# Other start addresses for the split activations and weights of a two-block kernel on one core

## The chip, the cores and the metric

The kernel runs on one NeuronCore of one Trainium2 chip. The metric is the device time of one execution in microseconds (us). The kernel before has a median of 3423.22 us over three runs (3422.39 to 3428.16).

## The reference

Two network blocks are applied to a sequence of 1024 tokens of width 1024 (and 256 context tokens), in float32. The first has a mixer with two branches (a chunked spatial MLP and a gated linear attention over chunks of 64) and a SwiGLU layer; the second has a linear recurrence with a short convolution, a banded attention with 16 heads, and again a SwiGLU layer. Cut to what matters here, it is a series of large products of activations with weights:

```python
u_l, v_l, q_l, k_l, vv_l, r_l, af_l, ab_l, ga_l, gb_l = jnp.split(h_lat @ w_in, offs, axis=-1)
...
x = x + g1 * mix_l
x = x + g2 * _swiglu(_modulate(_rmsnorm(x, norm2_g[l]), sh2, sc2), w_ffn_in[l], w_ffn_out[l])
...
def _swiglu(h, w_ffn_in, w_ffn_out):
    a, g = jnp.split(h @ w_ffn_in, 2, axis=-1)
    return (jax.nn.silu(g) * a) @ w_ffn_out
```

## The kernel before

Each float32 operand of a large product is split into two float32r parts, `hi` (a rounded copy, by ScalarE) and `lo` (the rest, a subtraction on GpSimd or VectorE). A product is then three matmuls for each 128 rows of the inner dimension: hi by hi, the activations' lo by the weights' hi, hi by the weights' lo. `gemm` (L158 to L167) does this with a weight tile as the stationary operand, 128 columns wide, and an activation tile of 512 columns as the moving one; `gemm_tok` (L169 to L177) has the activations as the stationary operand and 256 weight columns as the moving one. `product` in the first half of the feed-forward layer (L1051 to L1053) and in the second (L1264 to L1266) issue the same three matmuls inline.

The parts live in two pools. `hp` has 32 buffers named `hl`, of 512 float32r values in each partition (2048 bytes), which `part` and `hnew` hand out for activations; some activation parts are taken from other pools (`half`, 2048 bytes, and `slot`, 4096 bytes). `wp` has 4 buffers for each of two names, `wh` and `wl`, of 1024 values (4096 bytes), for weights: `unit` (L139 to L152) loads a weight block into a `raw` tile, copies it to `wh` and subtracts into `wl`; `parts` in the feed-forward layer (L1033) and `room` (L1195) take such a pair and use its two halves for two blocks. A pool's buffers stand back to back in each partition.

`wh[:, k]` is the weight block of inner index k. With a block width of 128 it begins 512 bytes behind the one before. One user has another width: `low_rank` (L553 to L562) multiplies with the gate weights `waf`, a `unit` of width 96, whose blocks begin 384 bytes apart; its loop is that of `gemm` with 8 values of k for each half of the tokens.

The order of the instructions on each engine is that in which the program issues them; which buffer a tile gets follows the order of requests. `bacc.Bacc` (L1856) reserves a scratch area of 16384 bytes in each partition at address 0 for DMA descriptors; with it, SBUF is full to within a few hundred bytes.

Of the kernel before, what the change touches and what calls it, by code (L numbers as in the profile page):

```python
# [10 lines left out]
F32R = mybir.dt.float32r  # L11
# [5 lines left out]
P = 128  # L17
# [14 lines left out]
HQ = 512  # L32
# [17 lines left out]
def hs(q):  # L50

    return slice(q * HQ, q * HQ + HQ)


class Prog:
# [54 lines left out]
        return self.gp.tile([P, HQ], dt, name="half")  # L110

    def part(self, dt=F32R):
        return self.hp.tile([P, HQ], dt, name="hl")

    def hnew(self, n=8):

        hi, lo = [[None, None] for _ in range(n)], [[None, None] for _ in range(n)]
        for q in QS:
            for k in range(n):
                hi[k][q] = self.hp.tile([P, HQ], F32R, name="hl")  # L120
                lo[k][q] = self.hp.tile([P, HQ], F32R, name="hl")
        return hi, lo

    def gnew(self, n, dt):
# [14 lines left out]
    def unit(self, src, kt=8, width=P, eng=None, raw=None, into=None):  # L139

        nc = self.nc
        self.loads += 1
        self.flush(False)
        n = kt * width
        v = lambda t: t[:, :n].rearrange("p (k c) -> p k c", c=width)
        r = v(self.raw.tile([P, 1024], F32, name="raw") if raw is None else raw)
        if src is not None:
            nc.sync.dma_start(r, src.rearrange("p (k c) -> p k c", c=width))
        hi, lo = (v(t) for t in into or [self.wp.tile([P, 1024], F32R, name=nm) for nm in ("wh", "wl")])
        nc.scalar.copy(hi, r)  # L150
        self.last_split = (eng or nc.gpsimd).tensor_tensor(lo, r, hi.bitcast(F32), op=ALU.subtract).ins  # L151
        return hi, lo  # L152
# [862 lines left out]
    def ffn_in(self, wi, hid):  # L1015


        nc = self.nc
        V = nc.vector
        add, sub = ALU.add, ALU.subtract  # L1020
        nf = FT

        def load(f, i, j):
            r = self.half()
            nc.sync.dma_start(r, wi[2 * f + i][:, hs(j)])
            return r

        def total(a, b, op):
            s = self.half()
            V.tensor_tensor(s, a, b, op=op)  # L1030
            return s

        def parts(*srcs):  # L1033
            hi, lo = (self.wp.tile([P, 1024], F32R, name=nm) for nm in ("wh", "wl"))
            out = []
            for i, s in enumerate(srcs):
                h, l = hi[:, hs(i)], lo[:, hs(i)]
                self.split(h, l, s, eng=nc.gpsimd)
                out.append([t.rearrange("p (k c) -> p k c", c=P) for t in (h, l)])
            return out  # L1040

        banks = [0]

        def product(w, n):
            mm = nc.tensor.matmul
            self.tick()
            banks[0] += 1
            o = self.mm_bank() if banks[0] % 2 else self.ax_bank()
            wh, wl = w
            for k, (h, l) in enumerate(self.X[n]):  # L1050
                mm(o, wh[:, k], h, start=k == 0, stop=False)  # L1051
                mm(o, wh[:, k], l, start=False, stop=False)  # L1052
                mm(o, wl[:, k], h, start=False, stop=k == 3)  # L1053
            return o

        def copied(a):
            t = self.half()
            nc.scalar.copy(t, a)
            return t

        def gate(a):
            s = self.t512()
            nc.scalar.activation(s, a, AF.Silu)
            return s

        def hidden(f, q, s, c):
            V.tensor_tensor(s, s, c, op=ALU.mult)
            self.store(hid[f][:, hs(q)], s)

        raws, todo, ready = {}, [], deque()  # L1070
        seen = [0]

        def ahead(f):

            self.loads += 1
            self.flush(False)
            for g in (f, f + 1):
                if g < nf and g not in raws and (g == f or f >= LEAD - 1):
                    raws[g] = [load(g, i, j) for i in QS for j in QS]
            a11, a12, a21, a22 = raws.pop(f)  # L1080
            s1 = total(a21, a22, add)
            s2 = total(s1, a11, sub)
            s3 = total(a11, a21, sub)
            s4 = total(a12, s2, sub)
            todo.extend([s2, s1, s3, a22, s4] if f < LEAD else [a11, s2, s1, s3, a22, a12, s4])

        def fill():
            while len(ready) < 7 and (todo or seen[0] < nf):
                while len(todo) < 2 and seen[0] < nf:
                    ahead(seen[0])  # L1090
                    seen[0] += 1
                ready.extend(parts(*todo[:2]))
                del todo[:2]

        def weights():
            fill()
            return ready.popleft()

        first = []
        for f, (w1, w2) in enumerate([parts(load(f, 0, 0), load(f, 0, 1)) for f in range(LEAD)]):  # L1100
            t = copied(product(w1, "B11"))
            s = total(t, product(w2, "B21"), add)
            nc.scalar.activation(s, s, AF.Silu)
            first.append((t, s))
            if not f:
                ahead(0)
                seen[0] = 1
        for f in range(nf):
            if f < LEAD:
                t, s0 = first[f]  # L1110
            else:
                t = copied(product(weights(), "B11"))
            u2 = total(t, product(weights(), "T2"), add)
            p5 = product(weights(), "T1")
            u3 = total(u2, product(weights(), "T3"), add)
            c22 = total(u3, p5, add)
            V.tensor_tensor(u2, u2, p5, op=add)
            V.tensor_tensor(u3, u3, product(weights(), "T4"), op=sub)
            if f >= LEAD:
                V.tensor_tensor(t, t, product(weights(), "B21"), op=add)  # L1120
                s0 = gate(t)
            hidden(f, 0, s0, u3)
            V.tensor_tensor(u2, u2, product(weights(), "B22"), op=add)
            hidden(f, 1, gate(u2), c22)

    def ffn_out(self, wo, hid, xs, scale, pieces, squares, norm, extra=lambda: iter(())):
# [3 lines left out]
        nc = self.nc  # L1130
# [64 lines left out]
        def room(w):  # L1195

            if not space:
                hi, lo = (self.wp.tile([P, 1024], F32R, name=nm) for nm in ("wh", "wl"))
                space.extend((hi[:, hs(i)][:, :w], lo[:, hs(i)][:, :w]) for i in QS)
            return space.pop(0)  # L1200

        def supply():

            for bi, ((kind, n), f0) in enumerate(zip(FF_BLOCKS, starts)):
# [17 lines left out]
                for p in range(4):  # L1222
                    self.loads += 1
                    self.flush(False)
                    raw = [self.raw.tile([P, 1024], F32, name="raw") for _ in QS]
                    for i in QS:
                        nc.sync.dma_start(raw[i][:, :n * P], wo[2 * p + i][:, cols])
                    (a11, a12), (a21, a22) = ((r[:, :w], r[:, w:2 * w]) for r in raw)

                    def done(src):  # L1230
                        hi, lo = room(w)
                        self.split(hi, lo, src, eng=nc.gpsimd)
                        return [t.rearrange("p (k c) -> p k c", c=P) for t in (hi, lo)], 1
                    yield done(a11)
                    yield done(a12)
                    s1 = self.t512()[:, :w]
                    V.tensor_tensor(s1, a21, a22, op=add)
                    V.tensor_tensor(a21, a11, a21, op=sub)
                    V.tensor_tensor(a11, s1, a11, op=sub)
                    V.tensor_tensor(a12, a12, a11, op=sub)  # L1240
                    for src in (s1, a11, a21, a22, a12):
                        yield done(src)
# [48 lines left out]
        for bi, (kind, nb) in enumerate(FF_BLOCKS[:-1]):  # L1291
# [19 lines left out]
            else:  # L1311
                for m in range(0, 8, 2):
                    t = self.t512()
# [553 lines left out]
```

## Time and profile before

| | |
|---|---|
| median of three runs | 3423.22 us |
| profiled execution, its own time | 3423.95 us |
| its span, first to last instruction | 3422.2 us |
| mean granted TensorE clock | 0.981 |
| TensorE matmul busy | 3260.1 us (95%), 15,868 |
| VectorE / ScalarE / GpSimd busy | 2126.6 / 1363.1 / 1539.2 us |
| DMA | 335.11 MB, mean 98 GB/s |

A matmul's length in the trace (0.39 us for 512 columns) is that of a pipelined instruction and overlaps the next one; the rate is read from the interval between starts. The rows PEld are TensorE's weight loads. A granted clock of 1.00 is 2.4 GHz, one of 0.50 is 1.2 GHz.

### The profile page before, as it was taken

The numbers are of one execution on the slowest core, as the hardware profiler recorded it, in microseconds if no ns is written. First come the engines' busy times: TensorE is split into PE (matmuls) and PEld (weight loads), VectorE is DVE, ScalarE is ACT, GpSimd is POOL, SyncE is SP. The second block draws the span as 40 slices with busy tenths as digits, with TensorE's granted clock in tenths as the row PEclk, the third lists the DMA queues.
The fourth block names the chain that finished last, engine by engine and source line by source line (L and its number), as shares of the span: only waits on it lengthen the run. The fifth ranks groups of instructions, "written<-read, shape, count | busy, mean of one in ns | idle before, by whom it ended". The sixth has DMA issues, their size and how long they took to land. (4 is left out here: it accounts for less than half of the span.)

```text
span 3422.2 us, 43238 instructions
## 1 busy us (share of the span) xinstructions
PE 3260.1 (95%) x15868; PEld 2695.3 (79%) x15868; DVE 2126.6 (62%) x3438; ACT 1363.1 (40%) x2396; POOL 1539.2 (45%) x991
## 2 busy tenths in 40 slices
PE   7999999999999999999989989999999999999998
PEld 4778888888888878888767867777777778888767
DVE  7554234333667386565798487777776585554786
ACT  4552122211122442222434486666665333233433
POOL 3222233221312775454655433444444775554764
PEclk9999999999999999999999999999999999999999
DMA  6121121244236522221342411111114422222342
GB/s 257 62 105 59 50 68 65 75 157 133 77 119 218 171 89 84 74 96 60 122 164 84 131 33 55 45 54 45 55 48 139 161 99 98 81 81 94 98 132 79
DMA packets 153012, 335.11 MB, mean 98 GB/s; under 512 B 20864, under 2 KB 29184, under 8 KB 152800
## 3 DMA queue, kind: packets, MB, share of 16 engines
q1 hardware_dynamic: 140640, 311.36, 27.5%
q10 hardware_dynamic: 12160, 20.98, 1.7%
q8 instruction: 126, 2.06, 0.3%
q14 instruction: 86, 0.70, 0.1%
HBM read 263.07 MB, written 69.21 MB: 97 GB/s over the span
## 5 line engine op out<-in xcount | busy, mean ns | idle before, releaser
L151 POOL TENSOR_TENSOR wl<-raw,wh 128x1024 fp32r<-128x1024 f32 (+1 forms) x188 | 426.1, 2271 | 742.7 <-ACT wh L150 666.1
L163 PE MATMUL mm<-hl,wh 128*128 128x512 f32 (+1 forms) x1584 | 636.8, 402 | 1.6 <-ACT t L1547 1.4
L165 PE MATMUL mm<-hl,wl 128*128 128x512 f32 (+1 forms) x1584 | 625.4, 395 | 2.8 <-POOL wl L151 2.8
L164 PE MATMUL mm<-hl,wh 128*128 128x512 f32 (+1 forms) x1584 | 624.2, 394 | 0.0
L193 POOL TENSOR_TENSOR wl<-half,wh 128x512 fp32r<-128x512 f32 x308 | 432.1, 1426 | 345.6 <-ACT wh L192 340.3
L150 ACT CAST wh<-raw 128x1024 fp32r<-128x1024 f32 (+3 forms) x189 | 177.3, 940 | 491.6 <-PE mm L164 215.7
L165 PEld LDWEIGHTS mm<-hl,wl 128*128 128x128 f32 (+1 forms) x1584 | 300.9, 190 | 68.0 <-POOL wl L151 3.6
L163 PEld LDWEIGHTS mm<-hl,wh 128*128 128x128 f32 (+1 forms) x1584 | 301.6, 190 | 59.5 <-ACT t L1547 1.8
L164 PEld LDWEIGHTS mm<-hl,wh 128*128 128x128 f32 (+1 forms) x1584 | 301.3, 190 | 58.1 <-issue 0.5
L192 ACT CAST wh<-half 128x512 fp32r<-128x512 f32 x308 | 178.5, 619 | 390.4 <-PE ax L1052 197.2
L1030 DVE TENSOR_TENSOR half<-half 128x512 f32<-128x512 f32 x176 | 204.4, 1200 | 3.0
L1606 POOL TENSOR_SCALAR p<-p,ast 128x384 f32<-128x384 f32 (+1 forms) x64 | 84.1, 1314 | 263.5 <-DVE ast L1604 172.5
L175 PE MATMUL mm<-wh,hl 128*128 128x256 f32 x576 | 166.1, 289 | 3.4 <-ACT wh L150 3.4
L177 PE MATMUL mm<-wl,hl 128*128 128x256 f32 x576 | 164.5, 286 | 1.9 <-POOL wl L151 1.9
L176 PE MATMUL mm<-wh,hl 128*128 128x256 f32 x576 | 164.5, 286 | 0.8 <-DVE hl L193 0.6
L1052 PE MATMUL mm<-hl,wh 128*128 128x512 f32 x360 | 140.6, 391 | 3.3 <-POOL hl L193 3.3
L1051 PE MATMUL mm<-hl,wh 128*128 128x512 f32 x360 | 140.3, 390 | 0.7 <-ACT hl L192 0.7
L1053 PE MATMUL mm<-hl,wl 128*128 128x512 f32 x360 | 140.3, 390 | 0.0
L1051 PE MATMUL ax<-hl,wh 128*128 128x512 f32 x344 | 134.2, 390 | 2.0 <-ACT hl L192 1.3
L1053 PE MATMUL ax<-hl,wl 128*128 128x512 f32 x344 | 134.1, 390 | 0.1
L1052 PE MATMUL ax<-hl,wh 128*128 128x512 f32 x344 | 133.9, 389 | 0.0
L193 POOL TENSOR_TENSOR wl<-raw,wh 128x384 fp32r<-128x384 f32 x96 | 113.1, 1198 | 39.4 <-ACT wh L192 38.8
(419 smaller groups left out, 7996.7 us busy)
## 6 DMA issues: line engine op xcount, KB each, us to landing
half<-in_w_fi SPq DMA_DIRECT2D x196, 256.0 KB, 4.8
hid<-t SPq DMA_DIRECT2D x78, 256.0 KB, 2.0
half<-hid SPq DMA_DIRECT2D x72, 256.0 KB, 4.5
raw<-in_w_ada SPq DMA_DIRECT2D x32, 512.0 KB, 3.8
raw<-in_w_o SPq DMA_DIRECT2D x32, 512.0 KB, 3.9
raw<-in_w_fo SPq DMA_DIRECT2D x32, 384.0 KB, 3.3
slot<-in_w_ada SPq DMA_DIRECT2D x16, 512.0 KB, 10.2
raw<-in_w_u SPq DMA_DIRECT2D x16, 512.0 KB, 3.7
```

Source lines behind the costliest of these rows:

```text
L150: nc.scalar.copy(hi, r)
L151: self.last_split = (eng or nc.gpsimd).tensor_tensor(lo, r, hi.bitcast(F32), op=ALU.subtract).ins
L163: mm(o, wh[:, k], h[k][q][:, s], start=k == 0, stop=False)
L164: mm(o, wh[:, k], l[k][q][:, s], start=False, stop=False)
L165: mm(o, wl[:, k], h[k][q][:, s], start=False, stop=k == kt - 1)
L175: mm(o, h[k][q][:, s], wh[:, k % 4], start=k == 0, stop=False)
L192: self.nc.scalar.copy(hi, x)
L193: (eng or self.nc.vector).tensor_tensor(lo, x, hi.bitcast(F32), op=ALU.subtract)
L1030: V.tensor_tensor(s, a, b, op=op)
L1051: mm(o, wh[:, k], h, start=k == 0, stop=False)
L1052: mm(o, wh[:, k], l, start=False, stop=False)
L1053: mm(o, wl[:, k], h, start=False, stop=k == 3)
```

## The change

Each buffer of `hp` becomes 12 values longer and each buffer of `wp` 16 values longer, and the tiles use only the first 512 or 1024 of them. So the buffers are spaced by 2096 and 4160 bytes, where they were spaced by 2048 and 4096. The descriptor scratch is halved to 8192 bytes, which gives the room for the padding. No instruction is added, removed or moved. Where a tile of either pool is asked for, the request goes through `part` or the new `wpart`.

```diff
     def part(self, dt=F32R):
-        return self.hp.tile([P, HQ], dt, name="hl")
+        return self.hp.tile([P, HQ + 12], dt, name="hl")[:, :HQ]
+
+    def wpart(self, name):
+        return self.wp.tile([P, 1024 + 16], F32R, name=name)[:, :1024]
...
-                hi[k][q] = self.hp.tile([P, HQ], F32R, name="hl")
-                lo[k][q] = self.hp.tile([P, HQ], F32R, name="hl")
+                hi[k][q], lo[k][q] = self.part(), self.part()
...
-        hi, lo = (v(t) for t in into or [self.wp.tile([P, 1024], F32R, name=nm) for nm in ("wh", "wl")])
+        hi, lo = (v(t) for t in into or [self.wpart(nm) for nm in ("wh", "wl")])
...
-            hi, lo = (self.wp.tile([P, 1024], F32R, name=nm) for nm in ("wh", "wl"))
+            hi, lo = (self.wpart(nm) for nm in ("wh", "wl"))
...
-    nc = bacc.Bacc("TRN2", target_bir_lowering=False, num_devices=1)
+    nc = bacc.Bacc("TRN2", target_bir_lowering=False, num_devices=1, dynamic_dma_scratch_size=8192)
```

The same replacement stands in `room`.

## Rows read from the trace of the kernel before

**Rows 1.** The page's first part: busy us (share of the span) and instructions by engine.

```profile
PE 3260.1 (95%) x15868; PEld 2695.3 (79%) x15868; DVE 2126.6 (62%) x3438; ACT 1363.1 (40%) x2396; POOL 1539.2 (45%) x991
```

**Rows 2.** Stretches: us, busy PE, PEld, DVE, ACT, POOL, granted clock, DMA share, GB/s.

```profile
1280.00:1600.00 320.00, 320.00 (x1413) 265.08 (x1412) 189.59 (x223) 94.14 (x167) 163.56 (x120) 1.00 0.24 81
1960.00:2600.00 640.00, 593.60 (x2844) 484.72 (x2843) 483.91 (x982) 438.16 (x827) 266.60 (x149) 0.97 0.16 50
...
2051.20:2053.80 2.60, 2.60 (x8) 2.00 (x7) 2.56 (x4) 1.41 (x2) 1.44 (x1) 0.50 0.00 0
1450.20:1455.90 5.70, 5.70 (x27) 4.69 (x25) 2.45 (x4) 1.68 (x3) 2.91 (x2) 1.00 0.04 14
```

**Rows 3.** Instructions in order of time (start us, length us), a steady stretch.

```profile
1450.23 0.39 PE L1051 MATMUL ax<-hl,wh 128*128 128x512 f32 x1
1450.23 0.19 PEld L1052 LDWEIGHTS ax<-hl,wh 128*128 128x128 f32 x1
...
1455.90 0.39 PE L1052 MATMUL ax<-hl,wh 128*128 128x512 f32 x1
```

**Rows 4.** In order of time, a stretch at the half clock.

```profile
2051.21 0.63 PE L163 MATMUL mm<-hl,wh 128*128 128x512 f32 x1
...
2053.77 0.63 PE L163 MATMUL mm<-hl,wh 128*128 128x512 f32 x1
```

**Rows 5.** TensorE's groups by line and shape: count, busy us, mean ns, idle before.

```profile
L163 PE MATMUL mm<-hl,wh 128*128 128x512 f32 x1568 | 630.5, 402 | 1.6 <-ACT t L1547 1.4 <-ACT wh L150 0.2
...
L1051 PE MATMUL ax<-hl,wh 128*128 128x512 f32 x344 | 134.2, 390 | 2.0 <-ACT hl L192 1.3 <-DVE half L1030 0.7
...
L1051 PE MATMUL ax<-half,wh 128*128 128x512 f32 x272 | 106.4, 391 | 0.0
```

**Rows 6.** In order of time, `low_rank` with 96 weight columns.

```profile
103.14 0.40 PE L163 MATMUL mm<-hl,wh 128*96 128x512 f32 x1
103.38 0.40 PE L164 MATMUL mm<-hl,wh 128*96 128x512 f32 x1
...
105.92 0.40 PE L163 MATMUL mm<-hl,wh 128*96 128x512 f32 x1
106.16 0.40 PE L164 MATMUL mm<-hl,wh 128*96 128x512 f32 x1
```

**Rows 7.** In order of time, 512-column products behind a run of other matmuls.

```profile
252.00 0.40 PE L163 MATMUL mm<-hl,wh 128*128 128x512 f32 x1
252.24 0.39 PE L164 MATMUL mm<-hl,wh 128*128 128x512 f32 x1
252.46 0.39 PE L165 MATMUL mm<-hl,wl 128*128 128x512 f32 x1
...
254.07 0.39 PE L163 MATMUL mm<-hl,wh 128*128 128x512 f32 x1
...
255.43 0.39 PE L163 MATMUL mm<-hl,wh 128*128 128x512 f32 x1
```

**Rows 8.** In order of time, products between the attention's small matmuls.

```profile
2097.41 0.40 PE L163 MATMUL ax<-slot,wh 128*128 128x512 f32 x1
...
2098.56 0.40 PE L165 MATMUL ax<-slot,wl 128*128 128x512 f32 x1
```

**Rows 9.** In order of time, products with 256 moving columns.

```profile
245.77 0.28 PE L175 MATMUL mm<-wh,hl 128*128 128x256 f32 x1
...
246.95 0.28 PE L176 MATMUL mm<-wh,hl 128*128 128x256 f32 x1
...
249.95 0.28 PE L177 MATMUL mm<-wl,hl 128*128 128x256 f32 x1
```

**Rows 10.** ScalarE's copies into the two pools, by line and shape.

```profile
L192 ACT CAST wh<-half 128x512 fp32r<-128x512 f32 x308 | 178.5, 619 | 390.4 <-PE ax L1052 197.2 <-issue 148.4 <-DVE half L1030 23.0
...
L192 ACT CAST hl<-half 128x512 fp32r<-128x512 f32 x76 | 45.9, 617 | 50.7 <-DVE half L1176 23.3 <-DVE half L338 11.4 <-DVE half L1181 7.0
```

**Rows 11.** The page's DMA queues: kind, packets, MB, share of 16 engines.

```profile
q1 hardware_dynamic: 140640, 311.36, 27.5%
q10 hardware_dynamic: 12160, 20.98, 1.7%
```

More of the change, by code (lines that the diff above doesn't have):

```diff
@@ L1197, in room @@
             if not space:
-                hi, lo = (self.wp.tile([P, 1024], F32R, name=nm) for nm in ("wh", "wl"))
+                hi, lo = (self.wpart(nm) for nm in ("wh", "wl"))
                 space.extend((hi[:, hs(i)][:, :w], lo[:, hs(i)][:, :w]) for i in QS)
```

## The prediction

> **What bounds the kernel now.** I read the busy times first, then a table of stretches, then single matmuls in order of time in the stretches where nothing is waited for. TensorE is busy for 3260.1 of 3422.2 us; VectorE has 62%, GpSimd 45%, ScalarE 40% [rows 1]. In the stretch 1280 to 1600 us TensorE has all 320.00 us while the next busiest engine has 189.59; in 1960 to 2600 it has 593.60 of 640 and VectorE 483.91, so some waiting is mixed in there [rows 2]. In steps of 40 us, 35 of 86 stretches are like the first. The chain of waits adds nothing: its last links are a short tail. So the time is mostly the number of matmuls times the interval from one matmul's start to the next, and a change of addresses alone, with the same instructions in the same order, can reach the time only through that interval, or through longer instructions on the engines that feed it.
>
> The interval in the steady stretch: from 1450.23 to 1455.90 us there are 25 intervals, (1455.90 - 1450.23) / 25 = 226.8 ns; each weight load starts together with the matmul before the one that needs it (both at 1450.23) and takes 0.19 us, so it is read from SBUF while that matmul streams its moving operand [rows 3]. The granted clock is 1.00 there, 2.4 GHz [rows 2], and 512 columns at 2.4 GHz are 213.3 ns, so some 13.4 ns of each interval are something else. Where the granted clock is 0.50, 1.2 GHz [rows 2], this is gone: six intervals from 2051.21 to 2053.77 are 426.7 ns each, exactly 512 / 1.2 [rows 4]. So the excess is not a fixed charge for each instruction in ns. It fits two reads that get into each other's way only when the engine streams at full speed, which is the case in which addresses could matter.
>
> **What the change touches.** The big kinds of matmul with a moving operand of 512 columns are L163 to L165 (1568 each with moving `hl`) and L1051 to L1053 (344 each with `hl` into `ax`, 272 with `half`, and as many again into `mm`) [rows 5]; with the smaller kinds of that shape in the same view they come to about 11,000 of the 15,868 matmuls. Nearly all have `wh` or `wl` as weights, and most have `hl` as the moving operand. Before, every buffer of the two pools begins at the same remainder modulo 512 bytes (spacings 2048 and 4096, slices by k 512 bytes apart). After, the remainder steps by 48 bytes from one `hl` buffer to the next, and by 64 bytes between weight buffers. Within one product the weights keep their remainder over k, `wh` and `wl` differ, and the moving one alternates between the two parts and moves on with k.
>
> **Where the trace shows other remainders.** One place: `low_rank` takes its weights 96 columns wide, so `wh[:, k]` steps by 384 bytes, and modulo 512 it runs through four remainders and repeats after 4 k, which is 12 matmuls. There the intervals do not settle. The twelve from 103.14 to 105.92 us take 2.78 us, 231.7 ns each, for narrower weights; and the lengths repeat with just that period: a pair with 0.40 us stands at 103.14 and 103.38, and the next such pair in the same place of the loop at 105.92 and 106.16, 2.78 us later, while matmuls in between show 0.39 [rows 6]. What has the period of 4 k in that loop is the weights' remainder alone. The second witness is a restart. After a run of other matmuls, with every remainder equal, the intervals are uneven for about nine matmuls, (254.07 - 252.00) / 9 = 230.0 ns, and then lock: (255.43 - 254.07) / 6 = 226.7 ns [rows 7]. Where the attention's small matmuls lie between, they never lock: (2098.56 - 2097.41) / 5 = 230.0 ns [rows 8]. So 226.7 is a settled state that is lost when the relation between the two reads is disturbed, and the unsettled state costs 3.3 to 5.0 ns more. After the change that relation is another one at nearly each step. For a moving operand of 256 columns the sign is the other way: unsettled (246.95 - 245.77) / 10 = 118 ns, settled (249.95 - 246.95) / 25 = 120 ns [rows 9]. It concerns some 1,900 matmuls (L175 to L177 and their like).
>
> **Sum.** Of the 11,000 about one in five is already unsettled (an estimate: the attention's 640 us hold 2844 of 15,868 matmuls, 18% [rows 1, 2], and restarts add a little). That leaves 8,800. At 230.0 they cost 8,800 x 3.3 = 29 us, at 231.7 they cost 8,800 x 5.0 = 44 us. I take 3.7 ns, nearer to the restart, since that has weights of the same 128 columns: 33 us. The 256-column ones give back 1,900 x 2 = 4 us. In the stretches where TensorE waits, part of a longer interval only shortens the wait; of the 29 us left I take off a tenth: 26. Bounds for a single interval are the uneven ones themselves: about 0.22 us (252.24 to 252.46) and 0.24 (252.00 to 252.24) [rows 7]. If all 11,000 went to 0.22 us the kernel would gain 11,000 x 6.7 = 74 us, if all went to 0.24 it would lose 11,000 x 13.3 = 146; no run of matmuls here stays at either, so these are outer bounds and not ends of the range.
>
> **What costs nothing.** ScalarE's copy into `wh` (128x512) takes 619 ns and the one into `hl` 617 [rows 10], the same for tiles of two pools; they lie under TensorE's work, as ScalarE is busy for 94.14 and GpSimd for 163.56 of the 320 us from 1280 [rows 2]. If each were 5% longer, that cover would still hold; where TensorE waits for a split (1960 to 2600) it would not, which at 5% of ScalarE's 438.16 us there is 22 us at the very most, and I see no reason for it. Pools, buffer counts, order of allocation and waits stay as they are, so no transfer starts at another point. The halved descriptor scratch makes room for the padding (32 x 48 + 8 x 64 = 2048 bytes); 140,640 of the 153,012 packets are on one hardware queue (q1, named hardware_dynamic), 12,160 on another like it [rows 11], and I cost it at nothing, with nothing gained either.
>
> **The skill against this.** The row shows that intervals depend on the weights' remainder. The Trainium skill says otherwise: "TensorE: Matmul & The Clock Gate", step-by-step of part 2, has two independent SBUF read ports for TensorE, so that loading the next weights takes no bandwidth from the running matmul, and "SBUF — State Buffer", section "Who interferes with whom", has TensorE never waiting on another engine. By that rule addresses would not matter and the time would stay at 3423; that is the first rival. The restart speaks for it, being uneven with equal remainders; the 12-matmul period speaks against it.
>
> **Rivals.**
> 1. Nothing changes (the padding doesn't do what it is for): the period of twelve is a property of 96-column weights, and the lock doesn't depend on addresses. For it: products with `hl` and with `half`, tiles in quite different places, have the same length in the mean, 390 and 391 ns [rows 5]. Against it: narrower weights alone give no reason for a period of 4 k. 3420 to 3428 us. Chance 0.22.
> 2. Faster: with unequal remainders the two reads meet less often, and the interval for 512 columns falls below 226.7, as the unsettled 256-column one falls below 120. Place: all products with `wh` and `wl`. Price: 2 ns as there, times 11,000 = 22 us, 3402. It decides from the point where the mean interval in the 1280 to 1600 stretch is under 226 ns. If the excess of 13.4 ns went altogether, as at the half clock, it would be 147 us (3277), and half of that if all stood at 0.22 us; no run at full clock comes near. Chance 0.20, 0.04 of it for these larger forms.
> 3. The lock survives within each product, because the weights keep their remainder there and the pairs of remainders repeat in order, and is only lost for a third of the matmuls: 29 / 3 = 10 us, 3434. Chance 0.16.
>
> **How the numbers follow.** Forecast: the lock is lost. The profiled execution took 3423.95 us around its span of 3422.2, 0.7 over the median of 3423.22; 3423.95 + 26 = 3450. Chance 0.42, own range 3440 to 3485, its upper end being 226.7 to 233 ns for all that is now locked (8,800 x 6.3 = 55 us) and a few us more. The range for all cases, 3402 to 3480, takes in no change and the small gain and leaves out the large gain and the worst loss, under 2 in 10. Under 0.2%, about 7 us, a measurement of this kernel can't be told from no change. Faster 0.20, same 0.22, slower 0.58.
>
> **What would show it.** Right: from 1280 to 1600 us (now 320.00 us of TensorE, all settled) the same 1413 matmuls take some 325 us, with intervals spread between 0.22 and 0.24 us and no lock; copies and splits keep their mean lengths; the clock stays 1.00 there. Rival 1: 226.7 ns as now. Rival 2: a mean under 226. Rival 3: uneven intervals only for a few matmuls at the head of each product. Wrong altogether if instructions of VectorE, ScalarE or GpSimd have other lengths, or waits on the feeding engines grow.

## The result, and the profile after

| | before | after |
|---|---|---|
| median of three runs, us | 3423.22 | 3444.12 (3442.51 to 3445.69) |
| profiled execution, its own time, us | 3423.95 | 3442.51 |
| its span, us | 3422.2 | 3440.7 |
| mean granted clock | 0.981 | 0.985 |

The ratio is 1.0057, with a 95% interval of 1.0034 to 1.008: slower by 21 us at the median and by 18.5 us in the span. The forecast was 3450, its own range 3440 to 3485. All 15,868 TensorE instructions run in the same order as before. Line numbers are two higher after: L165 to L167 are the old L163 to L165, L177 to L179 the old L175 to L177, and L1053 to L1055 the old L1051 to L1053.

First the page's busy line of the kernel after (busy us, share, instructions), beside [rows 1]:

```profile
PE 3283.1 (95%) x15868; PEld 2683.0 (78%) x15868; DVE 2126.6 (62%) x3438; ACT 1363.3 (40%) x2396; POOL 1543.2 (45%) x991
```

TensorE has grown by 23.0 us and GpSimd by 4.0; VectorE is the same to the tenth. The stretches of [rows 2], after:

```profile
1280.00:1600.00 320.00, 320.00 (x1385) 260.08 (x1384) 189.37 (x222) 91.66 (x162) 160.84 (x116) 1.00 0.24 82
...
1960.00:2600.00 640.00, 595.54 (x2844) 482.40 (x2844) 487.17 (x967) 437.11 (x817) 268.88 (x148) 0.98 0.15 49
```

In the first, which has no waits and a full clock, 1385 matmuls fit where 1413 did: each takes longer. In the second, with its waits, as many fit as before, 2844. There the granted clock was also a little higher, 0.98 against 0.97, so that line alone doesn't say whether the waits or the clock made up for the longer intervals; the table at the end of this section parts the two. Single matmuls in order of time (start us, length us), beside [rows 3]:

```profile
1453.01 0.39 PE L1054 MATMUL mm<-half,wh 128*128 128x512 f32 x1
...
1457.09 0.39 PE L1054 MATMUL ax<-half,wh 128*128 128x512 f32 x1
...
1457.55 0.40 PE L1053 MATMUL mm<-half,wh 128*128 128x512 f32 x1
...
1459.88 0.39 PE L1054 MATMUL mm<-half,wh 128*128 128x512 f32 x1
```

The interval is no longer one number. From 1453.01 it is (1457.09 - 1453.01) / 18 = 226.7 ns, as before; with the next weight buffer, from 1457.55, it is (1459.88 - 1457.55) / 10 = 233 ns. Over the matmuls that ran from 1280 to 1600 us before, the mean is 231.2 where it was 226.67. The groups of [rows 5] (mean ns of one), a 256-column stretch beside [rows 9], and ScalarE's copy into `wh` beside [rows 10]:

```profile
L165 PE MATMUL mm<-hl,wh 128*128 128x512 f32 x1568 | 633.2, 404 | 1.4 <-ACT t L1549 1.4
...
L1053 PE MATMUL ax<-half,wh 128*128 128x512 f32 x272 | 107.0, 393 | 0.0
```

```profile
249.10 0.28 PE L178 MATMUL mm<-wh,hl 128*128 128x256 f32 x1
...
251.93 0.28 PE L178 MATMUL mm<-wh,hl 128*128 128x256 f32 x1
```

```profile
L194 ACT CAST wh<-half 128x512 fp32r<-128x512 f32 x308 | 178.4, 618 | 403.9 <-PE ax L1054 209.6 <-issue 150.5 <-PE mm L166 19.7
```

Matmuls fed from `hl` and from `half` have both grown by some 2 ns in the length shown, though `half` was not moved: their weights were. With 256 columns the interval is (251.93 - 249.10) / 24 = 117.9 ns, where it was 120. The copy takes 618 ns where it took 619. At the half clock nothing has changed (beside [rows 4]): six intervals of (2063.65 - 2061.09) / 6 = 426.7 ns, exactly as before.

```profile
2061.09 0.63 PE L167 MATMUL mm<-hl,wl 128*128 128x512 f32 x1
...
2063.65 0.63 PE L167 MATMUL mm<-hl,wl 128*128 128x512 f32 x1
```

Where the time went, by stretches of the time before, matmul by matmul. "512 columns" and "256 columns" are the growth of all such intervals at full clock (215 to 245 ns, or 106 to 130 ns, in both traces), with the number of the first kind ahead of it. "Half clock" is the growth of all other intervals that a half-clock stretch touches in either trace, and "rest" that of what is left, nearly all of it intervals with a wait. "Shift" is by how much later the same matmuls run at the end of the stretch than at its start; it is the sum of the four, to rounding. All columns but the second are in us.

| stretch, us | intervals | 512 columns | 256 columns | half clock | rest | shift |
|---|---|---|---|---|---|---|
| 0 to 680 | 1378 | +4.3 | -1.9 | +1.6 | -0.4 | +3.5 |
| 680 to 960 | 705 | +2.5 | -1.7 | -1.1 | -0.3 | -0.5 |
| 960 to 1600 | 2661 | +11.3 | 0.0 | 0.0 | -0.4 | +10.8 |
| 1600 to 2800 | 3657 | +11.6 | -0.2 | -6.4 | -6.8 | -1.8 |
| 2800 to 3120 | 1412 | +6.3 | 0.0 | 0.0 | 0.0 | +6.3 |
| 3120 to the end | 913 | +3.5 | -0.3 | -2.5 | -0.5 | +0.3 |
| all | 10,726 | +39.4 | -4.1 | -8.4 | -8.4 | +18.6 |

The stretches in which TensorE hardly waits (960 to 1600 and 2800 to 3120 us, most of the two feed-forward layers) pass the growth on. The attention and what lies around it, 1600 to 2800 us, pass on none of it, for two reasons of like size: shorter waits, and less time at the half clock.

### The profile page after: what moved, and what is told of

It reads as the page before. It is cut to its first block, busy times and chain, and to the rows that moved or that the text cites. A ratio compares the mean times of both kernels' runs of the same rounds, so it can differ in the third digit from the quotient of the medians.

```text
span 3440.7 us, 43238 instructions
## 1 busy us (share of the span) xinstructions
PE 3283.1 (95%) x15868; PEld 2683.0 (78%) x15868; DVE 2126.6 (62%) x3438; ACT 1363.3 (40%) x2396; POOL 1543.2 (45%) x991
## 5 line engine op out<-in xcount | busy, mean ns | idle before, releaser
L165 PE MATMUL mm<-hl,wh 128*128 128x512 f32 (+1 forms) x1584 | 639.5, 404 | 1.4 <-ACT t L1549 1.4
L167 PE MATMUL mm<-hl,wl 128*128 128x512 f32 (+1 forms) x1584 | 627.7, 396 | 2.5 <-POOL wl L153 2.5
L167 PEld LDWEIGHTS mm<-hl,wl 128*128 128x128 f32 (+1 forms) x1584 | 299.8, 189 | 71.6 <-POOL wl L153 3.3
L165 PEld LDWEIGHTS mm<-hl,wh 128*128 128x128 f32 (+1 forms) x1584 | 300.2, 190 | 63.1 <-ACT t L1549 1.8
L177 PE MATMUL mm<-wh,hl 128*128 128x256 f32 x576 | 165.0, 287 | 3.3 <-ACT wh L152 3.3
L179 PE MATMUL mm<-wl,hl 128*128 128x256 f32 x576 | 163.4, 284 | 1.6 <-POOL wl L153 1.6
L1053 PE MATMUL mm<-hl,wh 128*128 128x512 f32 x360 | 141.8, 394 | 0.6 <-ACT hl L194 0.6
L1055 PE MATMUL mm<-hl,wl 128*128 128x512 f32 x360 | 141.6, 393 | 0.0
L1053 PE MATMUL ax<-hl,wh 128*128 128x512 f32 x344 | 135.8, 395 | 1.4 <-ACT hl L194 1.0
L1055 PE MATMUL ax<-hl,wl 128*128 128x512 f32 x344 | 135.4, 394 | 0.0
```

Of the source, the lines that this page charges most:

```text
L165: mm(o, wh[:, k], h[k][q][:, s], start=k == 0, stop=False)
L167: mm(o, wl[:, k], h[k][q][:, s], start=False, stop=k == kt - 1)
L177: mm(o, h[k][q][:, s], wh[:, k % 4], start=k == 0, stop=False)
```

## The experiments

In all kernels but the two small ones the computation is the whole one. A weight buffer's start minus a moving buffer's start, modulo 256 bytes, is called the difference below; before, it is 0 for all products in question. The `hl` buffers of the changed kernel lie 2112 bytes apart, not the 2096 that were asked for; the intervals of the kernel with only the activations spaced show it, below. So all differences in the changed kernel are multiples of 64: 0, 64, 128 or 192.

### One difference at a time

Small kernel: it leaves the computation out and only issues groups of 48 matmuls on three tiles, groups following without a break, at a granted clock of 1.00 in all the rows shown. For each number of columns, `g` moves the weights 16 bytes further from group to group:

```python
for n in (512, 256):
    for g in range(32):
        group(n, [(W, 128 * (i % 8) + 4 * g, H, 512 * (i % 2)) for i in R])
```

> A kernel of its own, which leaves out the whole computation: 74 groups of 48 matmuls (float32r, 128 weight columns), a one-column float32 matmul ahead of each group. Group 1 warms up; groups 2 to 33 have 512 moving columns and weights that begin 0, 16, ..., 496 bytes (modulo 512) behind the remainder of the moving operand, the same for all 48; groups 34 to 65 the same with 256 moving columns; 66 and 67 shift both operands alike; 68 steps the weights' remainder by 64 bytes from matmul to matmul, 69 the moving operand's, 70 both; 71 alternates the weights by 256 bytes, 72 puts the lo weights 256 bytes off in the order hi, hi, lo; 73 has 96 columns in blocks 384 bytes apart, 74 the same in blocks 512 apart, 75 128 columns in blocks 384 apart. Theory A (the difference of the two remainders sets the interval): 226.7 ns for difference 0, other values between 224 and 236 for others, each constant within its group. Theory B (only a change of the difference from one matmul to the next unsettles the lock): 226.7 ns in all groups 2 to 33, 66 and 67, and 230 to 232 in 68 to 70, 73 and 75; 226.7 or less in 74. Theory C (addresses don't matter, 96 columns do): 226.7 everywhere except 73 and 74, which agree at 231.7.

Rows of equal matmuls are put together in the trace (start, time of all of them, their count); each row lies inside one group: difference 0, 64 and 192 bytes; weights stepping by 64 bytes from matmul to matmul; 96 columns in blocks 384 bytes apart; 96 columns in blocks 512 apart; 128 columns in blocks 384 apart; then 256 columns at 0 and 64 bytes.

```profile
61.70 10.59 PE L37 MATMUL ps<-act,wt 128*128 128x512 f32 x46
...
105.86 10.43 PE L37 MATMUL ps<-act,wt 128*128 128x512 f32 x44
...
193.63 10.70 PE L37 MATMUL ps<-act,wt 128*128 128x512 f32 x46
...
620.43 10.59 PE L37 MATMUL ps<-act,wt 128*128 128x512 f32 x45
...
675.62 10.60 PE L37 MATMUL ps<-act,wt 128*96 128x512 f32 x45
...
686.75 10.51 PE L37 MATMUL ps<-act,wt 128*96 128x512 f32 x45
...
697.79 10.37 PE L37 MATMUL ps<-act,wt 128*128 128x512 f32 x44
```

```profile
417.24 5.44 PE L37 MATMUL ps<-act,wt 128*128 128x256 f32 x44
...
440.12 5.26 PE L37 MATMUL ps<-act,wt 128*128 128x256 f32 x45
```

The first says (10.59 - 0.39) / 45 = 226.7 ns, the second (10.43 - 0.39) / 43 = 233.5 by the rounded row and 233.2 over the whole group. Over the groups: 226.7 ns at 0 and 16 bytes, 233 to 234 from 32 to 160 except 232 at 80, 229.9 at 176, 228.9 at 192, 233.3 at 208 and 224, 226.7 at 240; from 256 bytes on the same series again. Shifting both operands by 64 or by 192 bytes leaves 226.7, so it is the difference that counts and not an address. With 256 columns the order is another: 120.0 at 0, 113.3 at 64 and 192, 116.6 to 120 elsewhere. So rival 1 falls: addresses do set the interval.

The prediction's first witness, [rows 6], turns out to mix two causes. With 96 columns and *equal* remainders, blocks 512 bytes apart, the interval is 230.0 ns; with 96 columns and blocks 384 apart it is 231.9; and with 128 columns and blocks 384 apart it is (10.37 - 0.39) / 43 = 232.1. So the narrower weights alone cost 3.3 ns, the stepping blocks alone 5.4, and both together 5.2: they don't add, and the 5.0 ns of [rows 6] can't be shared out between them. In the changed kernel `low_rank` runs as before, (105.90 - 103.12) / 12 = 231.7 ns by the rounded rows.

The groups in which the difference steps show one thing more. Weights that step by 64 bytes from matmul to matmul take 231.7 ns, where the mean of the four constant differences 0, 64, 128 and 192 is 230.5; blocks 384 apart have the differences 0 and 128 in turn and take 232.1, where the mean of those two is 230.1. So a changing difference costs 1 to 2 ns there beyond what the single differences cost. Stepping the moving operand, or both, gives 232.0 and 231.7; weights that alternate by 256 bytes settle at 226.7.

### The parts of the change, one by one

```diff
-        return self.wp.tile([P, 1024 + 16], F32R, name=name)[:, :1024]
+        return self.wp.tile([P, 1024], F32R, name=name)
```

This leaves only the activations spaced; the next leaves only the weights spaced, and the third spaces the weights by a whole 512 bytes, so that all differences stay 0, with the halved scratch and the new placement kept.

> Only the activation buffers are padded; the weight buffers keep their spacing of 4096 bytes. Under theory B the moving operand's remainder changes with nearly each matmul, so nearly the whole loss is there: 3438 to 3446 us. If the loss comes from the weights' remainders alone: 3423. Under theory C 3423 as well.

```diff
-        return self.hp.tile([P, HQ + 12], dt, name="hl")[:, :HQ]
+        return self.hp.tile([P, HQ], dt, name="hl")
```

> Only the weight buffers are padded, by 64 bytes; the activation buffers keep their spacing of 2048. The remainder is constant over k within wh and within wl, and wh and wl lie 256 bytes apart in it. Under theory A a loss of its own size for each buffer, 3430 to 3446 us. Under theory B only the change between wh and wl is left, one in three matmuls: 3428 to 3438. If the loss comes from the moving operand alone: 3423.

```diff
-        return self.hp.tile([P, HQ + 12], dt, name="hl")[:, :HQ]
+        return self.hp.tile([P, HQ], dt, name="hl")
...
-        return self.wp.tile([P, 1024 + 16], F32R, name=name)[:, :1024]
+        return self.wp.tile([P, 1024 + 128], F32R, name=name)[:, :1024]
```

> The weight buffers are padded by 512 bytes, the activation buffers not at all, and the scratch is halved as in the changed kernel: other spacings and places, the same remainders everywhere. Theories A and B: 3420 to 3427 us, intervals locked at 226.7 ns. A rival in which the halved scratch or the moved pools cost the time: 3436 to 3446.

| | ratio to before | 95% interval | mean 512-column interval, 1280 to 1600 us |
|---|---|---|---|
| only activations spaced | 1.0046 | 1.0033 to 1.006 | 229.2 ns |
| only weights spaced | 1.0056 | 1.0044 to 1.0069 | 230.6 ns |
| weights spaced by 512 bytes | 1.0005 | 0.9996 to 1.0013 | 226.67 ns |
| the change again, another chip | 1.0062 | 1.005 to 1.0074 | 231.2 ns |

So neither the scratch nor the places in memory cost anything that shows, and either half of the change alone costs most of the whole: the two don't add, which fits a loss that depends on the difference of the two addresses. The stretch of the third kernel is that of [rows 2] again:

```profile
1280.00:1600.00 320.00, 320.00 (x1414) 264.96 (x1413) 190.61 (x223) 94.43 (x167) 164.92 (x120) 1.00 0.24 82
```

The kernel with only the weights spaced lets one see the differences at work. There every moving buffer has one remainder modulo 256, and the four buffers of `wh`, and of `wl`, have the differences 0, 64, 128 and 192 in turn. In the feed-forward layer a buffer serves two products of 12 matmuls. The first matmuls of five buffers' products in order of time:

```profile
1300.46 0.40 PE L1053 MATMUL mm<-half,wh 128*128 128x512 f32 x1
...
1306.05 0.39 PE L1053 MATMUL mm<-hl,wh 128*128 128x512 f32 x1
...
1311.64 0.39 PE L1053 MATMUL mm<-hl,wh 128*128 128x512 f32 x1
...
1317.14 0.39 PE L1053 MATMUL mm<-half,wh 128*128 128x512 f32 x1
...
1322.60 0.40 PE L1053 MATMUL mm<-hl,wh 128*128 128x512 f32 x1
```

Each step over 24 matmuls: 5.59, 5.59, 5.50 and 5.46 us, that is 232.9, 232.9, 229.2 and 227.5 ns, and then the same four again, all along the stretch. In that cyclic order the small kernel gave 233.2 (64), 233.4 (128), 228.9 (192) and 226.7 (0). Their mean is 230.5, against 230.6 in this kernel and 231.2 with the whole change. With only the activations spaced, the products fed from `hl` (704 of 1232 by the counts of [rows 5]) see all four and those fed from `half` see 0: 0.57 x 230.5 + 0.43 x 226.7 = 228.9, against 229.2. Its trace also shows the two apart: from 1280 to 1600 us the matmuls fed from `hl` take 231.1 ns in the mean and those fed from `half` 226.9.

The kernel with only the activations spaced tells two more things. `gemm` takes the `hl` buffers in pairs, two for each k, and its intervals there repeat every six matmuls, that is every four buffers: 236, 226, 232, 226, 231, 229 ns from 696.9 us on. Four buffers are what a spacing of 2112 bytes gives, 64 modulo 256; at 2096 the remainders would repeat only after 16 buffers. And a changing difference costs something here too. From 1108.6 to 1148.0 us 168 intervals in a row, again with a period of six, have a mean of 234.4 ns, more than any of the four differences has by itself (233.4 at most). Two matmuls in there, 24 intervals apart, at (1119.86 - 1114.23) / 24 = 234.6 ns:

```profile
1114.23 0.40 PE L165 MATMUL mm<-hl,wh 128*128 128x512 f32 x1
...
1119.86 0.40 PE L165 MATMUL mm<-hl,wh 128*128 128x512 f32 x1
```

The change was also run once more as it is:

> The changed kernel once more, on the same chip as the three others. Theory A: the mean of the differences 0, 64, 128 and 192, and steps between them, 230 to 232 ns for 512 columns, and 0.5 to 0.7% slower: 3434 to 3442 us.

It gave the ratio in the table's last row, as expected, a span of 3443.2 us, and the same intervals. Its 3444.97 us lie above the expected 3434 to 3442, as the kernel before also takes longer on that chip (3422.67 us against 3417.72).

### All weights moved by one constant distance

Each of the next three moves every weight part by the same number of bytes, so that nothing alternates: 16, 96 and 64 bytes (4, 24 and 16 values). The edit for 64:

```diff
-        return self.wp.tile([P, 1024 + 16], F32R, name=name)[:, :1024]
+        return self.wp.tile([P, 1024 + 64], F32R, name=name)[:, 16:1040]
```

with `hl` unpadded as above. The weight buffers are then spaced by 4352 bytes, a multiple of 256.

> All weight tiles begin 16 bytes into buffers spaced by 4352 bytes, the activation buffers keep 2048, so every product with wh or wl has the difference 16 (modulo 256). Theory A by the sweep (226.7 ns at 0 and 16 for 512 columns; 118.4 instead of 120.0 for 256): same as before, 3414 to 3421 us, with 226.7 ns in the stretch 1280 to 1600. A rival in which any start off a multiple of 64 bytes costs the engines that write or read these tiles: 3430 or more.

> All weight tiles begin 96 bytes into their buffers: the difference is 96 everywhere and constant. Theory A by the sweep (234.2 ns for 512 columns): 7.5 ns on each locked matmul, so the stretch 1280 to 1600 grows by 320 x 7.5 / 226.7 = 10.6 us, and the kernel by 28 to 40 us, to 3446 to 3458. Theory B (only changes cost): 3418 us and 226.7 ns, as the difference never changes.

> All weight parts begin 64 bytes later, so every 512-column product has the same difference of 64 bytes, and nothing alternates. Theory C (a change of the difference from matmul to matmul keeps the products from settling, and a constant 64 settles like 0 after a restart): the stretch 1280 to 1600 stays at 320 us with 226.7 ns, time within 0.2% of before. Theory D (the interval belongs to the difference modulo 256, 233.2 ns at 64, as in the first sweep): the stretch takes 329 us, and the time grows by 25 to 45 us, 0.7 to 1.3%. Theory E (a constant difference also costs because each product enters it from another state): something between, with a period that repeats.

| constant difference | ratio to before | 95% interval | 512-column interval, 1280 to 1600 us |
|---|---|---|---|
| 16 bytes | 1.0067 | 1.0051 to 1.0083 | 233.3 ns |
| 64 bytes | 1.0098 | 1.0085 to 1.0112 | 233.3 ns |
| 96 bytes | 1.0129 | 1.0116 to 1.0142 | 234.3 ns |

The 16 bytes were a miss: no loss was expected, as the small kernel had 226.7 there, and the loss is 23 us. The 96 bytes lose more than was expected, though their interval is the expected one. The 64 bytes decide between "a changing difference keeps the products from settling" and "each difference has its own interval". The same stretch, and then two matmuls 15 intervals apart:

```profile
1280.00:1600.00 320.00, 320.00 (x1373) 257.82 (x1372) 186.44 (x220) 92.06 (x162) 157.90 (x115) 1.00 0.24 81
```

```profile
1319.69 0.39 PE L1053 MATMUL mm<-half,wh 128*128 128x512 f32 x1
...
1323.19 0.40 PE L1053 MATMUL ax<-half,wh 128*128 128x512 f32 x1
```

(1323.19 - 1319.69) / 15 = 233.3 ns, with no change of the difference from matmul to matmul, and it stays so in a pattern that repeats (236, 231, 236, 230, 236, 231 ns). So 233.3 is as settled as 226.7 is. In the main, what the change does is not to disturb a lock: it gives three quarters of the matmuls a difference whose own interval is longer. The mean of the four, 230.5, makes up 3.8 of the 4.5 ns that the changed kernel lost in this stretch. The other 0.7 fit the steps from matmul to matmul; no run of the whole kernel tried those by themselves.

### Behind a restart

Small kernel, computation left out: groups of 24 matmuls in the kernel's order (hi by hi, lo by hi, hi by lo), each behind 1, 2 or 4 plain float32 matmuls, differences from 0 to 240 bytes.

```python
for i, (w, h) in enumerate(((W, H), (W, L), (V, H))):
    s, m = ((h, hc), (w, wc)) if tok else ((w, wc), (h, hc))
```

> A kernel of its own, which leaves out the whole computation: groups of 24 matmuls in the order of gemm (512 moving columns) and then of gemm_tok (256), the weight tiles shifted by 0, 16, ..., 240 bytes against the activations, each shift three times, behind 1, 2 and 4 plain float32 matmuls of 128 columns. Theory A with a memory (the difference modulo 256 bytes decides together with the state in which a group begins): for 512 columns 226.7 ns behind every restart at 0, 226.7 behind some and 233.3 behind others at 16 and 240, 229 to 234 at the rest; for 256 columns 113.3 behind some restarts and some 118 behind others at 64 and 192. Rival (no memory; the 233.3 of the kernel with 16 bytes comes from the order hi, hi, lo over two weight tiles): the three restarts agree at each shift, with 233.3 at 16.

One group at 64 bytes (from 121.66 us on) and one at 16 (from 64.83 on):

```profile
121.66 0.39 PE L43 MATMUL ps<-act,wu 128*128 128x512 f32 x1
...
124.38 0.39 PE L43 MATMUL ps<-act,wu 128*128 128x512 f32 x1
```

```profile
64.83 0.39 PE L43 MATMUL ps<-act,wu 128*128 128x512 f32 x1
...
69.72 0.40 PE L43 MATMUL ps<-act,wu 128*128 128x512 f32 x1
```

At 64 bytes (124.38 - 121.66) / 12 = 226.7 ns, where the sweep and the whole kernel have 233.3; at 16 bytes (69.72 - 64.83) / 21 = 233 ns, where the sweep had 226.7 and the whole kernel 233.3. Behind these restarts the results repeat with 64 bytes: 226.7 at 0, 64, 128 and 192, 233.3 at 16, 228.9 at 48. So at 16 and at 64 bytes the engine can settle at either of two intervals. The whole kernel with a constant 16 bytes shows both of them as well, though the stretch of the table has only one. About one in five of its undisturbed runs of 12 intervals is at 226.7 ns, and the same lines on tiles of the same names have now one, now the other:

```profile
753.11 0.39 PE L166 MATMUL mm<-slot,wh 128*128 128x512 f32 x1
...
755.83 0.39 PE L166 MATMUL mm<-slot,wh 128*128 128x512 f32 x1
```

```profile
764.45 0.40 PE L167 MATMUL mm<-slot,wl 128*128 128x512 f32 x1
...
767.95 0.40 PE L167 MATMUL mm<-slot,wl 128*128 128x512 f32 x1
```

These are (755.83 - 753.11) / 12 = 226.7 and (767.95 - 764.45) / 15 = 233.3 ns. What picks one of the two is not shown. For 512 columns the three restarts agree at every difference to within 0.5 ns, which is what the rival without a memory expected; and the two small kernels differ in the order of their tiles as well as in what ran before. The order of the three matmuls can't be all of it, as the whole kernel has the same order in the two stretches above. A difference of 0, once settled, gave 226.7 in every run. For 256 columns, 0 and 64 bytes gave 120.0, and 48 bytes 113.3 behind 1 and 4 plain matmuls and 117.75 behind 2: there only what ran before differs, and it does decide.

### Using the gain of the 256-column products

`gemm_tok` has the weights as the moving operand. Only its weight blocks (width 256) are moved, by 64 bytes, and in a second kernel by 48 (12 values); everything else has difference 0.

```diff
+    def wpart(self, name, o=0):
+        return self.wp.tile([P, 1024 + 64], F32R, name=name)[:, o:o + 1024]
...
+        hi, lo = (v(t) for t in into or [self.wpart(nm, 16 if width == 256 else 0) for nm in ("wh", "wl")])
```

> Only the weight tiles that are the moving operand of 256 columns (the wide pairs of gemm_tok) begin 64 bytes into their buffers; all others keep difference 0. Theory A by the sweep (113.3 ns instead of 120.0 at a difference of 64 for 256 columns, 226.7 kept for 512): 1,920 matmuls x 6.7 ns = 13 us off TensorE's time, of which some is lost in waits: 3406 to 3412 us, faster than both kernels. Theory C: no change, 3418.

> Only the weights of the products with 256 moving columns begin 48 bytes later, all else is as in the kernel before. Behind restarts a difference of 48 bytes gave 113.3 ns twice and 117.75 ns once, where 64 bytes gave 120.0. If 113.3 holds: some 1,900 matmuls x 6.7 ns = 13 us less, 3410, and 3412 after a loss where TensorE waits. If 117.75 holds: 4 us less, 3419, as with 64 bytes. If what counts is not the difference but only a step of the weights' own address: no change from 120.0 and 3423.

With 64 bytes the ratio is 0.9987 (0.9979 to 0.9996), with 48 bytes 0.9996 (0.9987 to 1.0005). The hoped-for 113.3 ns did not come: two matmuls 36 intervals apart, with 64 bytes,

```profile
223.74 0.28 PE L179 MATMUL mm<-wl,hl 128*128 128x256 f32 x1
...
227.98 0.28 PE L179 MATMUL mm<-wl,hl 128*128 128x256 f32 x1
```

are (227.98 - 223.74) / 36 = 117.8 ns apart in the mean, and with 48 bytes the mean over the kernel is 118.4. So the size of the gain was a miss in both: with 64 bytes 4 us came, where 6 to 12 were expected; with 48 bytes 1 us, where 11 to 13 were expected if 113.3 ns held and 4 if 117.75 did, and it can't be told from no gain. By its ratio the kernel with 64 bytes is the fastest of this study, 3418.3 against 3422.67 us for the kernel before on the same chip, but by less than 0.2%.

## Why the prediction was right, point by point

**The bound.** Right in the main. The same instructions ran in the same order, the lengths on the other engines stayed but for small shifts, and the loss came through the interval between matmuls. What the bound left out is the granted clock, which differed between the two profiled executions.

**The excess is absent at the half clock.** Right, also after: 426.7 ns with unequal differences.

**What the change touches.** The steps were put at 48 bytes for `hl`; they are 64, because of the rounded spacing. By the spacing that made the differences 0, 64, 128 and 192, each for about a quarter, and none in between.

**"226.7 is a settled state that is lost when the relation is disturbed."** As the main mechanism this step failed, though its size was near. What costs is the difference itself: a constant 64 bytes, with nothing to disturb it, is a steady 233.3 ns, and with only the weights spaced each buffer's 24 matmuls take the interval of their difference. The changed kernel still has stretches at 226.7, where the forecast looked for none. Steps from matmul to matmul cost too, but less: by the sum above some 0.7 of the 4.5 ns. The first witness [rows 6] mixed the stepping blocks with the narrower weights, either of which alone gives 230 ns or more. Nor does its period of twelve come from the remainder alone: in the sweep the effect repeats with 256 bytes, and modulo 256 those blocks repeat after 2 k, six matmuls. The second, the restart [rows 7], shows how a settled interval is reached, not what an unequal difference costs.

**The price of one interval.** Taken at 3.7 ns, from 3.3 and 5.0. Measured in the stretch without waits: 231.2 - 226.67 = 4.5 ns, inside these bounds. Over all 512-column intervals at full clock the mean growth is 39.4 us / 10,726 = 3.7 ns; that it is just the figure taken is chance, since it averages stretches that were settled before with others that were not.

**The count.** One in five was taken out as already unsettled. But the attention's 512-column matmuls grew as well, from 229.3 to 231.8 ns. So not 8,800 at 3.7 = 33 us but 10,726 at 3.7 = 39.4 us is what the intervals lengthened by.

**The 256-column products.** 4 us back were forecast; the table has 4.1, from 1,920 of them at some 120 - 117.8 = 2.2 ns.

**What the waits hide.** The term that was mis-sized most. A tenth, 3 us, was taken off. The intervals' 39.4 less 4.1 is 35.3, and the matmuls came 18.6 us later at the end: 16.8 us, nearly half, are missing. The table parts them: 8.4 in intervals with waits, 8.4 in intervals that the half clock touches. Most of both lies from 1600 to 2800 us, where 3,657 intervals lengthened by 11.6 us and the work behind them came 1.8 us earlier. There TensorE waits for splits and for the attention's VectorE work, so a longer interval fills a wait. The prediction had the number for it in [rows 2], 593.60 of 640 us busy, 46 us of waits in one stretch, and took a tenth off the total instead of going by stretch. For the second cause it had no term: the profiled execution before spent 131.7 us at the half clock and the one after 102.7, most of the difference from 1600 to 2800 us. The kernel with only the weights spaced confirms the first: it too had 131.7 us at the half clock, its 512-column intervals grew by 35.8 us and its 256-column ones shrank by 4.6, and its span grew by 18.3, so 13 us were hidden without any difference of clock in the total, 12 of them in intervals with waits.

The two errors, +6.4 us in the intervals and -14 in what hides them, partly cancelled: 3450 forecast, 3444 measured. So the nearness of the number is in part luck.

**What costs nothing.** Right, by the kernel with 512 bytes: 1.0005 with the halved scratch and the new placement. The 4.0 us that GpSimd was busy longer after the change don't explain the loss: with a constant 64 bytes GpSimd has 1539.1 us, as before, and the time grows by more.

**The rivals.** Nothing changes: fell. With it falls, for this data type, the rule cited from the Trainium skill ("TensorE: Matmul & The Clock Gate", step-by-step of part 2) as it was read there, that with two independent read ports addresses wouldn't matter: the difference moves the interval from 226.7 to 233.3 ns. Whether it is the two reads that meet, no run shows. Faster: fell for 512 columns, where no difference in any run gave less than 226.6; its sign holds for 256 columns, 117.8 against 120.0. The lock survives within each product: its time, 3434, was short by 10 us, but its reason was the better one, since a product does settle while its difference stays, as the kernel with only the weights spaced shows; what it missed is that it settles at that difference's own interval.

**The marks.** The stretch from 1280 to 1600 us was to take some 325 us: its matmuls took 320 + 6.4. The clock there stayed at 1.00 and the copies kept their lengths, as said. Intervals with no lock at all were not what came: runs at 226.7 ns stand beside uneven ones.

## What to carry to other kernels

Where TensorE is busy all the time with float32r products, give stationary and moving buffers starts that are equal modulo 256 bytes, and look whether a pool rounds a padded size. Read the price of a longer interval stretch by stretch: what waits hide is most of it in one stretch and nothing in the next, so a share of the total is a poor guess; and compare the time at the half clock of the two profiles before giving the rest to waits. And before taking one loop as a witness for a cause, ask what else is special about it (here, 96 columns), and measure each of the two alone.

## What the runs showed of the hardware that was not expected

- The interval of float32r matmuls at full clock depends on the difference of the two operands' start addresses: 226.7, 228.9, 233.3 and 234.3 ns for 512 columns at 0, 192, 64 and 96 bytes. At the half clock it is 426.7 ns whatever the difference.
- It repeats with 256 bytes in the sweep without breaks and with 64 bytes behind restarts, and for 16 and 64 bytes two settled intervals, 226.7 and 233.3 ns, were seen. In the whole kernel a constant 16 gave both; a constant 64, once settled, gave only 233.3.
- A difference that changes from matmul to matmul costs 1 to 2 ns beyond the mean of the single differences in the small kernel (231.7 against 230.5, 232.1 against 230.1).
- For 256 columns the best difference is another one, 113.3 ns against 120.0 at 0, but it was not reached in the whole kernel.
- Weights of 96 columns take 230.0 ns at equal remainders, 3.3 more than those of 128.

What stays open: what in the chip makes the interval depend on the two addresses, and what picks between two settled intervals. No run here looked inside that. Nor is it known why the time at the half clock differs between runs, 102 to 132 us, among kernels with equal and with unequal differences alike.
